# A hybrid decoder layer on one core: the up-projection's products at fixed places in one PSUM pool

## The chip, the core and the metric

The kernel runs on one core of a Trainium2 chip. The metric is the device time of one execution in microseconds (us); lower is better. Five engines work side by side: TensorE (PE, matmuls; PEld is its weight load), VectorE (DVE), ScalarE (ACT), GpSimd (POOL) and SyncE (SP, which issues most DMAs). Each takes its own instructions in order and waits on semaphores that the others raise. Matmuls write to PSUM, which has eight banks of 128 x 512 fp32 values; DVE and ACT read them from there.

## The reference, cut to what matters

A sequence of 1024 tokens of width 1024 goes through one layer: RMSNorm, two attention branches, gates, a residual, and then the part that the change touches, the gated MLP with a causal convolution of width 3 over 2816 hidden channels:

```python
def conv_ffn(xn, w_up, conv_w, conv_b, w_down):
    u = xn @ w_up                                   # (1024, 5632)
    upad = jnp.pad(u, ((0, 0), (CONV_WIDTH - 1, 0), (0, 0)))
    c = conv_b
    for j in range(CONV_WIDTH):
        c = c + upad[:, j:j + S] * conv_w[j]
    gate, val = jnp.split(c, 2, axis=-1)
    return (jax.nn.silu(gate) * val) @ w_down
...
        xn = rmsnorm(x, norm_ffn_w[l])
        x = x + conv_ffn(xn, w_up[l], conv_w[l], conv_b[l], w_down[l])
```

## The kernel before, in words

Everything is held transposed: channels on the 128 partitions, the 1024 tokens along the free axis. An fp32 product is made of three fp32r matmuls: both operands are split into a high part (`...h`, a cast on ACT) and a low part (`...l`, a subtraction on DVE, L145 and L877), and high x high, high x low and low x high are added in PSUM.

The up-projection works on pairs of 128-channel blocks: pair j is gate block j and value block j + 22, for j = 0 to 21. Each pair's 2 x 2 block product is done by a Strassen-like scheme with seven products, P1 to P7, of 12 matmuls of 128x512 each (`product`, L957). The sums of weight blocks that this takes are `sa` and `sb` (made on POOL, L123 to L127), their high and low parts `sh` and `sl`; those of the plain blocks are `wh` and `wl`. The factor of the norm, `rstd`, is applied after the product. It comes from sums of squares (`ssq`, L223), a mean on DVE (`ms`, L230), a power on POOL (`rs`, L232), and eight transposes on PE (`spread`, L238) that bring it to all partitions in PSUM, from where ACT copies it in two halves into `rstd` (L1036).

Three stretches of `hidden` differ in how they hold the products.

- Pair 0 takes eight tiles `t` of one bank each from a pool `psF`: seven products and the sums of squares. `recombine` reads them (L515 to L523): L515 reads P1, L516 P2, L517 P6, L518 P7, L519 and L520 P5, L522 P3, L523 P4.
- Pairs 1 to 19 run in `steady`. `psF` is closed, and two pools take its banks: `psB` (four banks, tile `b`) and `psC` (two tiles `c` of two banks). A pair has three accumulators: b1 takes P1, then S2, S3 and A22 products on top of it; b2 takes P2; b3 takes S1 and S4. ACT copies what is in them between two products (L1108 s1, L1122 u2, L1124 s5 with tile name u, L1136 u3, L1094 or L1082 the last one), so that each product needs the copy before it. The tile of the transposes, `sp`, comes from `psC`. In the built program it lies in the two banks that P3 and P7 of pair 0 had.
- Pairs 20 and 21 take seven banks `t` each from a third pool, `psG2`. In the built program P1 of pair 20 lies in the bank of pair 19's b1.

While PE multiplies pair j, the other engines finish pair j - 1: the scale by `rstd` (L1213), the convolution's first tap on ACT (`taps` with n = 0, L1148, from `us` into a PSUM tile `c`), two taps on DVE (L1150), Silu (L1126), the product of the halves (L1128), and a store to `hd`. They also prepare the weights of pair j + 1. In `steady` the order on DVE, ACT and POOL is the order of the code (`in_order`); on PE and elsewhere a scheduler keeps the code's order as far as the inputs' estimated readiness lets it. With `reuse_waits="tile"` a tile in a reused place waits for the readers of the tiles that lay there.

Of the kernel before, what the change touches and what calls it, by code (L numbers as in the profile page):

```python
# [17 lines left out]
P = 128  # L18
# [26 lines left out]
class Trunk:  # L45
# [914 lines left out]
    def hidden(self, pair):  # L960
        nc, tc = self.nc, self.tc
        with ExitStack() as ctx:
            e = ctx.enter_context
            pctx = ExitStack()
            psF = self.psT = pctx.enter_context(tc.tile_pool(name="psF", bufs=8, space=PSUM, reuse_waits="tile"))
# [8 lines left out]
            for j in (0, NF - 2, NF - 1):  # L974
                w, ps = (ready.pop(j), {}) if j else (w0, {})
                if j == 0:

                    ps = {n: self.tl(psF, [P, H2], "t") for n in ("P1", "P2", "P5", "P7", "", "P6", "P3", "P4")}
                    ssq = ps.pop("")
# [22 lines left out]
                if j:  # L1002
                    ps = {n: self.tl(psF, [P, H2], "t") for n in (("P5", "P1", "P2", "P6", "P7", "P3", "P4") if j < NF - 1 else ("P1", "P2", "P5", "P6", "P7", "P4", "P3"))}
# [15 lines left out]
                if j == 0:  # L1019
# [7 lines left out]
                    pctx.close()  # L1027
                    with tc.tile_pool(name="psB", bufs=4, space=PSUM, reuse_waits="tile") as psB, \
                            tc.tile_pool(name="psC", bufs=2, space=PSUM, reuse_waits="tile") as self.psC:
                        b1, b2 = (self.tl(psB, [P, H2], "b") for _ in range(2))  # L1030
                        self.product(b1, st[1]["w"]["A11"], "B11", skip=True)
                        self.product(b2, st[1]["w"]["A12"], "B21", skip=True)
                        sp = self.tl(self.psC, [P, T], "c")
                        self.spread(sp, rs, 0, NB)
                        for hf in range(2):
                            self.mark_a = nc.scalar.copy(self.rstd[:, hf * H2:(hf + 1) * H2], sp[:, hf * H2:(hf + 1) * H2]).ins  # L1036
                        self.mark_v, self.mark_p = self.lo.ins, self.pow.ins
                        self.front, self.us = None, us
                        st[0] = {"us": us}
                        self.steady(st, (b1, b2), psB, tp, sums)  # L1040
                    psF = self.psT = e(tc.tile_pool(name="psG2", bufs=8, space=PSUM, reuse_waits="tile"))
# [27 lines left out]
    def steady(self, st, banks, psB, tp, sums):  # L1069
# [5 lines left out]
        with self.in_order(last):  # L1075
            c21 = None
            for j in range(1, NF - 1):
# [25 lines left out]
                if j > 1:  # L1103
                    b2 = self.tl(psB, [P, H2], "b")
                    self.product(b2, W["A12"], "B21", skip=True)
# [364 lines left out]
```

## Time and profile before

| | |
|---|---|
| median of 3 runs | 1329.02 us (1328.35 to 1329.96) |
| the profiled execution | 1328.19 us, of it span 1326.4 us |
| mean granted TensorE clock | 0.997 |
| PE busy | 1309.9 us, 99% of the span |
| DVE, ACT, POOL busy | 77%, 50%, 36% |
| PE's share of the chain that ended last | 94% |

The span is the time from the first to the last instruction; times in the order of time count from its start. A row of that order reads: start, duration, engine, line, operation, tile written <- tiles read, shape, and in brackets how long the engine had idled before it and what released it. Matmuls overlap: one of 128x512 is shown with 0.39 us, but the next starts 0.23 us after it. Buffer numbers are left out of names, so `b` is any of b1 to b3.

### The profile page before, as it was taken

The page shows a single profiled execution, that of the slowest core. Times are in us where ns is not written, and L with a number is a line of the kernel's source. Part 1 is how long each engine was busy: PE and PEld are TensorE (multiplying, and loading weights), DVE is VectorE, ACT ScalarE, POOL GpSimd, SP SyncE. Part 2 cuts the span into 40 slices and gives each one's busy share as a digit, 9 for nine tenths or more (in the row PEclk, how much of TensorE's full clock was granted, in tenths as well). Part 3 has the DMA queues.
Part 4 walks back from the last instruction along what each step waited for, and adds up shares of the span by engine and source line. Part 5 has one row for each costly group of instructions (what it writes and reads, how often), then busy time and mean ns, then how long its engine had stood idle before and what let it go on. Part 6 is the DMA issues. An engine that isn't in the chain of part 4 may idle for free.

```text
span 1326.4 us, 16954 instructions
## 1 busy us (share of the span) xinstructions
PE 1309.9 (99%) x6210; PEld 1091.4 (82%) x6210; DVE 1017.6 (77%) x1380; ACT 658.3 (50%) x1043; POOL 473.3 (36%) x364
## 2 busy tenths in 40 slices
PE   9999999999999999999998999999999999999997
PEld 7888888888888878888887888888888888888886
DVE  8846775289888976445668889888988897896865
ACT  9432232276667764333445454545454544554543
POOL 0446652000111015651436568656766632000002
PEclk9999999999999999999999999999999999999999
DMA  7334433976554236334433546745654127954534
GB/s 261 121 144 158 147 146 127 264 185 180 154 128 137 86 128 219 130 111 159 131 108 124 181 135 157 199 148 133 201 134 129 61 87 247 333 190 117 166 98 147
DMA packets 71586, 205.95 MB, mean 155 GB/s; under 512 B 8016, under 2 KB 15824, under 8 KB 71376
## 3 DMA queue, kind: packets, MB, share of 16 engines
q1 hardware_dynamic: 57472, 176.03, 40.8%
q0 software_dynamic: 2304, 11.54, 4.9%
q10 hardware_dynamic: 11728, 17.31, 3.6%
q8 instruction: 49, 0.80, 0.3%
q14 instruction: 33, 0.27, 0.1%
HBM read 156.08 MB, written 71.83 MB: 172 GB/s over the span
## 4 chain that ended last, share of the span: by engine, by line
PE 94%; DVE 2%; ACT 1%; issue 1%; DMA 0%; POOL 0%; SPq 0%; POOLq 0%; ACTq 0%; DVEq 0%
PE b L957 27%; PE t L957 16%; PE y L1283 9%; PE d L1283 7%; PE g L215 4%; PE g L216 4%; PE g L217 4%; PE sc L216 3%; PE sc L215 3%; PE sc L217 3%; PE sc L689 3%; PE t L705 1%; PE t L808 1%; PE sc L777 1%; PE t L717 1%; PE t L798 1%
## 5 line engine op out<-in xcount | busy, mean ns | idle before, releaser
L1213 POOL TENSOR_TENSOR us<-us,rstd 128x1024 f32<-128x1024 f32 x42 | 105.0, 2500 | 148.7 <-DVE us L1138 111.7
L196 DVE TENSOR_TENSOR wl<-raw,wh 128x1024 fp32r<-128x1024 f32 (+2 forms) x85 | 97.4, 1146 | 58.7 <-ACT wh L194 48.9
L194 ACT CAST wh<-raw 128x1024 fp32r<-128x1024 f32 (+2 forms) x85 | 74.2, 874 | 119.9 <-PE y L1283 50.7
L145 DVE TENSOR_TENSOR sl<-sf,sh 128x1024 fp32r<-128x1024 f32 x42 | 106.0, 2525 | 4.6 <-ACT sh L138 4.6
L232 POOL TENSOR_TENSOR rs<-ms,mhalf 128x8 f32<-128x8 f32 (+2 forms) x9 | 13.3, 1474 | 234.4 <-DVE ms L230 228.3
L1150 DVE SCALAR_TENSOR_TENSOR c<-us,vecs,c 128x1024 f32<-128x1024 f32 x76 | 95.6, 1279 | 0.7
L1283 PE MATMUL y<-h,wh 128*128 128x512 f32 (+1 forms) x324 | 95.2, 377 | 0.0
L1283 PE MATMUL d<-h,wh 128*128 128x512 f32 x264 | 81.3, 389 | 0.0
L215 PE MATMUL g<-xh,wh 128*128 128x512 f32 x176 | 71.0, 403 | 1.5 <-ACT g L618 1.5
L216 PE MATMUL g<-xl,wh 128*128 128x512 f32 x176 | 70.3, 400 | 0.0
L217 PE MATMUL g<-xh,wl 128*128 128x512 f32 x176 | 70.3, 399 | 0.0
L1283 PEld LDWEIGHTS y<-h,wh 128*128 128x128 f32 x324 | 59.4, 188 | 11.1
L1283 PE MATMUL y<-h,wl 128*128 128x512 f32 (+1 forms) x162 | 60.9, 376 | 0.0
L693 DVE CUSTOM_DVE_ANT_0 L<-sc,bias 128x128 f32<-128x128 f32 (+7 forms) x64 | 47.7, 752 | 17.0 <-PE sc L689 13.9
L672 POOL MEMSET aT<- 128x128 f32 x32 | 6.2, 206 | 151.7 <-PE t L718 98.0
L694 ACT ACTIVATE L<-L,sm 128x128 f32<-128x128 f32 (+7 forms) x64 | 49.6, 778 | 20.0 <-DVE sm L693 13.5
L1283 PEld LDWEIGHTS d<-h,wh 128*128 128x128 f32 x264 | 49.6, 188 | 10.4
L846 POOL TENSOR_TENSOR gr<-gr,rstd 128x1024 f32<-128x1024 f32 x16 | 40.3, 2520 | 46.7 <-DMA gr<-gd 39.0
L1283 PE MATMUL d<-h,wl 128*128 128x512 f32 x132 | 51.5, 390 | 0.0
L138 ACT CAST sh<-sf 128x1024 fp32r<-128x1024 f32 x42 | 44.3, 1054 | 13.3 <-POOL sf L124 12.0
L216 PE MATMUL sc<-ml,wh 128*128 128x512 f32 x128 | 49.9, 390 | 0.0
L215 PE MATMUL sc<-mh,wh 128*128 128x512 f32 x128 | 49.8, 389 | 0.0
(515 smaller groups left out, 4181.1 us busy)
## 6 DMA issues: line engine op xcount, KB each, us to landing
u<-qd SPq DMA_DIRECT2D x72, 256.0 KB, 6.6
raw<-in_w_up SPq DMA_DIRECT2D x23, 512.0 KB, 3.9
raw<-in_w_in SPq DMA_DIRECT2D x22, 512.0 KB, 3.8
hd<-c SPq DMA_DIRECT2D x22, 512.0 KB, 4.0
sdP<-in_w_down POOLq DMA_DIRECT2D x16, 704.0 KB, 8.6
rv<-in_w_up SPq DMA_DIRECT2D x21, 512.0 KB, 3.6
hc<-hd SPq DMA_DIRECT2D x33, 256.0 KB, 5.1
gr<-gd SPq DMA_DIRECT2D x16, 512.0 KB, 3.7
```

The costliest lines, as they stand in the source:

```text
L145: self.nc.vector.tensor_tensor(lo, src, hi.bitcast(F32), ALU.subtract)
L194: self.hi = nc.scalar.copy(wh, raw)
L196: self.lo = (eng or nc.vector).tensor_tensor(wl, raw, wh.bitcast(F32), ALU.subtract)
L215: nc.tensor.matmul(ps, wh[:, kc + o, :], ah, start=first and n == 0, stop=False)
L216: nc.tensor.matmul(ps, wh[:, kc + o, :], al, start=False, stop=False)
L217: nc.tensor.matmul(ps, wl[:, kc + o, :], ah, start=False, stop=last and n == len(kcs) - 1)
L693: nc.vector.tensor_tensor_reduce(L[:, :w], sc[:, lo:lo + w], self.bias[:, o:o + w], slope, 3e38, ALU.add, ALU.min, s[:, 0:1])
L694: nc.scalar.activation(L[:, :w], L[:, :w], AF.Exp, bias=s[:, 0:1], scale=-1.0, accum_out=s[:, 1:2] if c else self.s0[:, i:i + 1])
L957: nc.tensor.matmul(ps, (ah, ah, al)[p][:, k, :], (bh, bl, bh)[p], start=first and n == p == 0, stop=last and p == 2 and n == len(ks) - 1, ...
L1150: nc.vector.scalar_tensor_tensor(c, us[:, 2 - n:T + 2 - n], cw[2 - n], c, ALU.mult, ALU.add)
L1213: i = (nc.vector if m % NF == 0 else nc.gpsimd).tensor_tensor(us[:, 2:], us[:, 2:], self.rstd, ALU.mult)
L1283: nc.tensor.matmul(ps, v[:, k - k0, :], x, start=start and k == i == 0, stop=k == HK - 1 and i == 2, skip_group_check=True)
```

## The change

One pool, `psF`, with one buffer for each name, serves all 22 pairs. `bank(n)` gives the one-bank tile n0 to n3, and `banks(n)` gives the two halves of the two-bank tile c0 or c1: four banks and two times two. A tile is tracked as a whole, so whoever writes a half of c0 waits for what has read the other half.

- Pair 0: P1 in n0, P2 in n2, P7 in n1, P5 in n3, sums of squares and P6 in c0, P3 and P4 in c1.
- Pairs 1 to 19: b1 alternates between n0 and n1, b2 is n2, b3 is n3; the convolution's tiles are c0 for the gate half and c1 for the value half. The transposes write the two halves of c0, four for each, and ACT copies each half (now L1034).
- Pairs 20 and 21 use the same names. P1 of pair 20 is n1, P4 of it n0, which is pair 19's b1.
- In pair 1 (the second) the taps of pair 0 stand behind copies: the gate half's first tap behind u2 (L1128 in the changed kernel), the value half's behind s5 (L1132).

No instruction's work changes. The number of matmuls, copies, subtractions and DMAs stays.

On PE, pair 0's last two products: `t_6328` holds the sums of squares, `t_6329` is P6; in the changed kernel c_1085 is c0 (sums and P6), c_1086 is c1 (P4 here). Before:

```order
L223 MATMUL t_6328<-ones,rstd 128x1 x3
L957 MATMUL t_6329<-T_0h,sh_6312 128x512 [waits Activation_49]
L957 MATMUL t_6329<-T_0l,sh_6312 128x512 [waits DVE_49]
L957 MATMUL t_6329<-T_0h,sl_6314 128x512
L957 MATMUL t_6329<-T_1h,sh_6312 128x512 [waits Activation_49]
```

After:

```order
L223 MATMUL c_1085_6328<-ones,rstd 128x1 x3
L957 MATMUL c_1086_6329<-T_0h,wh_6320 128x512 [waits Activation_49]
L957 MATMUL c_1086_6329<-T_0l,wh_6320 128x512 [waits DVE_49]
L957 MATMUL c_1086_6329<-T_0h,wl_6322 128x512
L957 MATMUL c_1086_6329<-T_1h,wh_6320 128x512 [waits Activation_49]
L957 MATMUL c_1085_6328<-T_0h,sh_6312 128x512 [waits DVE_49]
L957 MATMUL c_1085_6328<-T_0l,sh_6312 128x512
```

Four matmuls of P4 moved ahead of P6, and P6's first matmul waits for a DVE instruction, which is the mean L230.

On PE, the transposes in pair 1 (`b_6502` is b1, now n_1110; `b_6503` is b2, now n_1111). Before:

```order
L957 MATMUL b_6503<-B_3h,wl_6473 128x512
L238 MATMUL c_6528<-ident,rs_6422 128x128 [waits DVE_49,Pool_49]
L238 MATMUL c_6528<-ident,rs_6422 128x128 x7
L957 MATMUL b_6502<-T_0h,sh_6476 128x512 [waits Activation_49]
L957 MATMUL b_6502<-T_0l,sh_6476 128x512
```

After:

```order
L957 MATMUL n_1111_6494<-B_3h,wl_6471 128x512
L238 MATMUL c_1112_6519<-ident,rs_6420 128x128 [waits DVE_49,Pool_49]
L238 MATMUL c_1112_6519<-ident,rs_6420 128x128 x3
L957 MATMUL n_1110_6493<-T_0h,sh_6474 128x512 [waits Activation_49]
L957 MATMUL n_1110_6493<-T_0l,sh_6474 128x512
L957 MATMUL n_1110_6493<-T_0h,sl_6475 128x512
L957 MATMUL n_1110_6493<-T_1h,sh_6474 128x512
L238 MATMUL c_1112_6519<-ident,rs_6420 128x128 [waits Activation_49]
L238 MATMUL c_1112_6519<-ident,rs_6420 128x128 x3
L957 MATMUL n_1110_6493<-T_1l,sh_6474 128x512
```

The DVE instruction waited for is L522 before and L517 after; four of the transposes moved behind four matmuls and wait for an ACT instruction, the copy of the first half.

On ACT in pair 1, from the cast of the third pair's `sa` on (`c_6558` and `c_6575` are pair 0's convolution tiles, `u_1118` is u2, `u_1119` is s5). Before:

```order
L138 CAST sh_6554<-sf_6492 128x1024 [waits Pool_49]
L1036 COPY rstd<-c_6528 128x512 [waits PE_49]
L1036 COPY rstd<-c_6528 128x512
L1148 ACTIVATE c_6558<-us_6448,vecs 128x1024 [waits DVE_49]
L1148 ACTIVATE c_6575<-us_6449,vecs 128x1024 [waits DVE_49,Activation_49]
L1122 COPY u_1118_6548<-b_6502 128x512 [waits PE_49]
L1124 COPY u_1119_6549<-b_6582 128x512 [waits PE_49]
L1126 ACT_TABLE_LOAD
```

After:

```order
L138 CAST sh_6545<-sf_6490 128x1024 [waits Pool_49]
L1034 COPY rstd<-c_1112_6519 128x512 [waits PE_49] x2
L1128 COPY u_1116_6539<-n_1110_6493 128x512 [waits DVE_49,PE_49]
L1162 ACTIVATE c_1125_6579<-us_6446,vecs 128x1024 [waits DVE_49]
L1132 COPY u_1117_6540<-n_1124_6565 128x512 [waits PE_49]
L1162 ACTIVATE c_1126_6594<-us_6447,vecs 128x1024 [waits DVE_49]
L1140 ACT_TABLE_LOAD
```

Each of the two first taps moved behind one copy. The diff:

```diff
@@ -961,8 +961,7 @@
         nc, tc = self.nc, self.tc
         with ExitStack() as ctx:
             e = ctx.enter_context
-            pctx = ExitStack()
-            psF = self.psT = pctx.enter_context(tc.tile_pool(name="psF", bufs=8, space=PSUM, reuse_waits="tile"))
+            self.psF = e(tc.tile_pool(name="psF", bufs=1, space=PSUM, reuse_waits="tile"))
             xc2 = e(tc.tile_pool(name="xc2", bufs=1, side="right", reuse_waits="tile"))
             self.uw = e(tc.tile_pool(name="uw", bufs=3, side="right", reuse_waits="tile"))
             prods = (("P1", "A11", "B11"), ("P2", "A12", "B21"), ("P5", "S1", "T1"), ("P7", "S3", "T3"),
@@ -975,8 +974,8 @@
                 w, ps = (ready.pop(j), {}) if j else (w0, {})
                 if j == 0:
 
-                    ps = {n: self.tl(psF, [P, H2], "t") for n in ("P1", "P2", "P5", "P7", "", "P6", "P3", "P4")}
-                    ssq = ps.pop("")
+                    ps = {n: self.bank(b) for n, b in (("P1", 0), ("P2", 2), ("P7", 1), ("P5", 3))}
+                    (ssq, ps["P6"]), (ps["P3"], ps["P4"]) = self.banks(0), self.banks(1)
                     for name, a, b in prods[:5]:
                         self.product(ps[name], w[a], b, range(3), last=False)
                     for k in range(4):
@@ -1000,7 +999,10 @@
                             self.hs[k] = self.split(h[:, 0], h[:, 1], raw[k // 2][:, k % 2 * H2:(k % 2 + 1) * H2])
                         lo = self.lo
                 if j:
-                    ps = {n: self.tl(psF, [P, H2], "t") for n in (("P5", "P1", "P2", "P6", "P7", "P3", "P4") if j < NF - 1 else ("P1", "P2", "P5", "P6", "P7", "P4", "P3"))}
+                    o = NF - 1 - j
+                    ps = {n: self.bank(b) for n, b in (("P1", (3, 1)[o]), ("P2", (1, 2)[o]), (("P5", 2), ("P4", 0))[o])}
+                    for i, names in enumerate((("P6", "P7"), ("P4", "P3")) if j == NF - 1 else (("P5", "P6"), ("P7", "P3"))):
+                        ps.update(zip(names, self.banks(i)))
                 for name, a, b in (prods[i] for i in ((0, 1, 2, 5, 3, 6, 4) if j == NF - 1 else (0, 1, 2, 5, 3, 4, 6) if j else (5, 6))):
                     self.product(ps[name], w[a], b, low=name == "P1")
                 us = [self.tl(tp, [P, T + 2], "us", bufs=3) for _ in range(2)]
@@ -1024,21 +1026,16 @@
                         self.whole(st[1], "g", "sa", "sb", "v")
                         st[2] = self.raw_pair(self.wsrc.pop(0)[0])
                         self.sums(st[2], "sa")
-                    pctx.close()
-                    with tc.tile_pool(name="psB", bufs=4, space=PSUM, reuse_waits="tile") as psB, \
-                            tc.tile_pool(name="psC", bufs=2, space=PSUM, reuse_waits="tile") as self.psC:
-                        b1, b2 = (self.tl(psB, [P, H2], "b") for _ in range(2))
-                        self.product(b1, st[1]["w"]["A11"], "B11", skip=True)
-                        self.product(b2, st[1]["w"]["A12"], "B21", skip=True)
-                        sp = self.tl(self.psC, [P, T], "c")
-                        self.spread(sp, rs, 0, NB)
-                        for hf in range(2):
-                            self.mark_a = nc.scalar.copy(self.rstd[:, hf * H2:(hf + 1) * H2], sp[:, hf * H2:(hf + 1) * H2]).ins
-                        self.mark_v, self.mark_p = self.lo.ins, self.pow.ins
-                        self.front, self.us = None, us
-                        st[0] = {"us": us}
-                        self.steady(st, (b1, b2), psB, tp, sums)
-                    psF = self.psT = e(tc.tile_pool(name="psG2", bufs=8, space=PSUM, reuse_waits="tile"))
+                    b1, b2 = self.bank(0), self.bank(2)
+                    self.product(b1, st[1]["w"]["A11"], "B11", skip=True)
+                    self.product(b2, st[1]["w"]["A12"], "B21", skip=True)
+                    for hf, sp in enumerate(self.banks(0)):
+                        self.spread(sp, rs, hf * 4)
+                        self.mark_a = nc.scalar.copy(self.rstd[:, hf * H2:(hf + 1) * H2], sp).ins
+                    self.mark_v, self.mark_p = self.lo.ins, self.pow.ins
+                    self.front, self.us = None, us
+                    st[0] = {"us": us}
+                    self.steady(st, (b1, b2), tp, sums)
                     w21 = st[NF - 1]
                     self.sums(w21, "sb")
                     self.whole(w21, "g", "sa", "sb", "v")
@@ -1066,7 +1063,14 @@
                     else:
                         self.defer.append(f)
 
-    def steady(self, st, banks, psB, tp, sums):
+    def bank(self, n):
+        return self.tl(self.psF, [P, H2], f"n{n}")
+
+    def banks(self, n):
+        t = self.tl(self.psF, [P, 2, H2], f"c{n}")
+        return t[:, 0], t[:, 1]
+
+    def steady(self, st, banks, tp, sums):
 
         nc, tc = self.nc, self.tc
         tt = nc.vector.tensor_tensor
@@ -1089,7 +1093,7 @@
                 if j == 1:
                     b1, b2 = banks
                 else:
-                    b1 = self.tl(psB, [P, H2], "b")
+                    b1 = self.bank((j + 1) % 2)
                     self.product(b1, W["A11"], "B11", skip=True)
                     nc.scalar.copy(half(old[1], 0), c21)
                     self.low(S, "sb")
@@ -1101,27 +1105,37 @@
                 for w in range(2):
                     self.scaled(m + w * NF, old[w])
                 if j > 1:
-                    b2 = self.tl(psB, [P, H2], "b")
+                    b2 = self.bank(2)
                     self.product(b2, W["A12"], "B21", skip=True)
                 s1, u2, s5, u3 = (self.tl(tp, [P, H2], n, bufs=1) for n in ("s1", "u2", "u4", "u3"))
                 us = S["us"] = [self.tl(tp, [P, T + 2], "us", bufs=3) for _ in range(2)]
                 nc.scalar.copy(s1, b1)
                 if j == 1:
                     self.whole(nxt, "sa")
-                c0 = self.taps(m, old[0], 0)
+                c0 = self.taps(m, old[0], 0) if j > 1 else None
                 self.product(b1, W["S2"], "T2", first=False, skip=True)
-                self.taps(m, old[0], 1, c0)
+                if j > 1:
+                    self.taps(m, old[0], 1, c0)
                 tt(half(us[0], 0), b2, s1, ALU.add)
-                self.taps(m, old[0], 2, c0)
-                c1 = self.taps(m + NF, old[1], 0)
-                self.taps(m + NF, old[1], 1, c1)
-                self.taps(m + NF, old[1], 2, c1)
+                if j > 1:
+                    self.taps(m, old[0], 2, c0)
+                    c1 = self.taps(m + NF, old[1], 0)
+                    self.taps(m + NF, old[1], 1, c1)
+                    self.taps(m + NF, old[1], 2, c1)
                 self.sums(nxt, "sb")
-                b3 = self.tl(psB, [P, H2], "b")
+                b3 = self.bank(3)
                 self.product(b3, W["S1"], "T1", skip=True)
                 nc.scalar.copy(u2, b1)
+                if j == 1:
+                    c0 = self.taps(m, old[0], 0)
                 self.product(b1, W["S3"], "T3", first=False, skip=True)
                 nc.scalar.copy(s5, b3)
+                if j == 1:
+                    c1 = self.taps(m + NF, old[1], 0)
+                    for n in (1, 2):
+                        self.taps(m, old[0], n, c0)
+                    for n in (1, 2):
+                        self.taps(m + NF, old[1], n, c1)
                 c = self.tl(self.cpl, [P, T], "c")
                 nc.scalar.activation(c, c0, AF.Silu)
                 self.whole(nxt, "g")
@@ -1144,7 +1158,7 @@
         nc = self.nc
         cw = [self.vecs[:, C_CW + 3 * m + k:C_CW + 3 * m + k + 1] for k in range(3)]
         if n == 0:
-            c = self.tl(self.psC, [P, T], "c")
+            c = self.tl(self.psF, [P, T], f"c{m // NF}")
             nc.scalar.activation(c, us[:, 2:], AF.Identity, bias=self.vecs[:, C_CB + m:C_CB + m + 1], scale=cw[2])
         else:
             nc.vector.scalar_tensor_tensor(c, us[:, 2 - n:T + 2 - n], cw[2 - n], c, ALU.mult, ALU.add)
```

## The prediction

> **What bounds the kernel now.** I read the page's table of engines first, then the list of what TensorE waited for, then the order of time around the two waits that the change touches.
>
> ```profile
> PE 1309.9 (99%) x6210; PEld 1091.4 (82%) x6210; DVE 1017.6 (77%) x1380; ACT 658.3 (50%) x1043; POOL 473.3 (36%) x364
> engine line waited for: us in total, times, longest us
> PE c L238 <- DVE us L522: 3.7, 1, 3.7
> ...
> PE t L957 <- ACT us L1082: 0.7, 1, 0.7
> ```
>
> PE is busy for 99% of the span, so the change can only win what PE idles or runs slowly. That list has ten rows. The first is by far the largest and is in the function that is changed; so is L1082's. No row of it names a product into `b`: the nineteen pairs between run without a wait. So there are two places to win at, and the question is what stands behind each.
>
> The first, in order of time (start, duration, engine, line, tile):
>
> ```profile
> 701.41 0.39 PE L957 MATMUL b<-B_3h,wl 128*128 128x512 f32 x1
> 702.83 0.68 DVE L519 TENSOR_TENSOR us<-t,u 128x512 f32<-128x512 f32 x1
> ...
> 704.63 0.68 DVE L522 TENSOR_TENSOR us<-t,u 128x512 f32<-128x512 f32 x1
> 705.45 1.07 PE L238 MATMUL c<-ident,rs 128*128 128x128 f32 x8 [3.65 <-DVE us L522]
> 706.26 0.69 PE L957 MATMUL b<-T_0h,sh 128*128 128x512 f32 x1
> 706.75 0.63 PE L957 MATMUL b<-T_0l,sh 128*128 128x512 f32 x1
> ...
> 710.46 0.39 PE L957 MATMUL b<-T_3h,sl 128*128 128x512 f32 x1
> 710.69 0.39 PE L957 MATMUL b<-T_0h,sh 128*128 128x512 f32 x1
> ```
>
> A full-speed matmul starts 0.23 us after the one before it (710.46, 710.69; over a row of them 0.2265), so PE could have gone on at 701.63. The eight transposes that spread the norm's factor go into a tile that lies over the banks of P3 and P7 of the first pair, and P3's last reader is L522: PE starts at 705.45. Behind the wait the matmuls start 0.42 to 0.49 us apart. The clock says why (columns: stretch, length, busy time of PE, PEld, DVE, ACT, POOL, granted clock, DMA share, GB/s):
>
> ```profile
> core 0: us, PE busy (x) PEld busy (x) DVE busy (x) ACT busy (x) POOL busy (x), PEclk, DMA share, GB/s
> 699.54:702.95 3.41, 2.26 (x10) 1.53 (x9) 3.41 (x4) 1.88 (x3) 2.33 (x2) 1.00 0.44 154
> 702.95:706.36 3.41, 0.91 (x9) 0.94 (x10) 2.95 (x5) 1.04 (x1) 3.41 (x3) 1.00 0.00 0
> 706.36:709.78 3.41, 3.41 (x11) 2.67 (x10) 2.11 (x2) 1.92 (x3) 0.67 (x1) 0.50 0.64 183
> ```
>
> After a stretch of 3.41 us with PE busy for 0.91 us (27%) the clock is halved for exactly one such stretch; after one with 2.26 us (66%) it was not. The S2 product's twelve matmuls take 710.69 - 706.26 = 4.43 us where 12 x 0.2265 = 2.72 would do: the half clock costs 1.71 us. The place thus costs 3.82 + 1.71 = 5.5 us.
>
> The second place, at the last but one pair:
>
> ```profile
> 1064.08 0.39 PE L957 MATMUL b<-T_3h,wl 128*128 128x512 f32 x1
> 1064.56 0.59 ACT L1082 COPY us<-b 128x512 f32<-128x512 f32 x1 [1.89 <-PE b L957]
> 1065.20 0.50 PE L957 MATMUL t<-B_0h,wh 128*128 128x512 f32 x1 [0.73 <-ACT us L1082]
> 1065.54 0.39 PE L957 MATMUL t<-B_0l,wh 128*128 128x512 f32 x1
> ```
>
> P1 of that pair takes the bank of the accumulator that the copy L1082 has yet to read. PE could have gone on at 1064.31, goes on at 1065.20, and the first matmul after a stop takes 0.34 instead of 0.23 us: 1.0 us.
>
> **The change part by part.** *Place 1, a new wait ahead of it.* The sums of squares and P6 now share one tile, so P6 may only start when the mean (DVE L230) has read the sums. PE puts four matmuls of P4 in front.
>
> ```profile
> 690.66 0.48 PE L957 MATMUL t<-T_0h,sh 128*128 128x512 f32 x1
> 690.98 0.40 PE L957 MATMUL t<-T_0l,sh 128*128 128x512 f32 x1
> 692.31 0.16 DVE L230 TENSOR_SCALAR ms<-t 128x8 f32<-128x8 f32 x1
> ```
>
> The four start at 690.66, 690.98, 691.21 and 691.44; the fifth could start at 691.66. L230 ends at 692.47, and PE follows a DVE result after 0.14 us (705.31 to 705.45 above): 692.61. That is 0.95 us of waiting and 0.1 for the restart, +1.05. DVE's queue ahead of L230 is the same, so the bounds are narrow, 0.9 to 1.15.
>
> *Place 1, the wait removed.* The next products are as many as before, so PE stands before the transposes at 701.63 + 1.05 = 702.68. Their tile now lies over the sums and P6; P6's reader L517 needs P6 (complete near 695.5) and moves behind the first `sl` subtraction, so it ends near 701.0: no wait. The wait for L522 goes.
>
> *Place 1, what is late next.* The transposes are now two groups of four into halves of one tile, and the second group waits until ACT has copied the first half. That copy stands on ACT behind a cast that waits for POOL:
>
> ```profile
> 700.54 1.29 POOL L123 TENSOR_TENSOR sf<-rv 128x512 f32<-128x512 f32 x1 [1.21 <-issue]
> 701.90 2.13 POOL L124 TENSOR_TENSOR sf<-sf,raw 128x512 f32<-128x512 f32 x1
> 704.07 1.04 ACT L138 CAST sh<-sf 128x1024 fp32r<-128x1024 f32 x1 [2.66 <-POOL sf L124]
> 706.56 1.08 ACT L1036 COPY rstd<-c 128x512 f32<-128x512 f32 x2 [1.44 <-PE c L238]
> ```
>
> POOL and DVE ahead of these have the same work, so the cast still ends at 705.11 and the copy (half of 1.08, begun at the cast's end) at 705.62; PE goes on at 705.75. Before that it does four transposes (half of 706.26 - 705.45: 0.41) and four matmuls (0.91), to 704.00. The new wait is 1.75 us. Then 0.41 for four transposes, 0.33 for the matmul after the stop and 7 x 0.2265: the S1 product starts at 708.1 instead of 710.69. Against 3.82 + 0.81 + 4.43 = 9.06 us before stand 0.41 + 0.91 + 1.75 + 0.41 + 1.92 = 5.40, plus the 1.05: a gain of 2.6 us. Bounds: L124 takes 2.13 us where its neighbour takes 1.29; at 1.29 the wait shrinks by 0.84, and a second such slow instruction ahead of it would add 0.84. I take the row as it stands. The sum holds no half clock; the rival below prices that.
>
> *The second pair's order on ACT.* The copies u2 and u4 (L1122, L1124; u4 is the tile of s5) go ahead of the two convolution starts (L1148). Without it the starts, 2.4 us together, would hold u2 back and the S3 product with it; with it u2 is read near 708.9, before S3's turn at 710.8. But the value half's start now stands between u4 and the chain that leads to the third pair's weights:
>
> ```profile
> 708.93 2.41 ACT L1148 ACTIVATE c<-us,vecs 128x1024 f32<-128x1024 f32 x2 [1.29 <-DVE us L1213]
> 713.21 0.39 PE L957 MATMUL b<-T_3h,sl 128*128 128x512 f32 x1
> 713.63 0.59 ACT L1124 COPY u<-b 128x512 f32<-128x512 f32 x1 [1.78 <-PE b L957]
> 714.24 1.28 ACT L1126 ACT_TABLE_LOAD   x1
> 715.53 1.03 ACT L1126 ACTIVATE c<-c 128x1024 f32<-128x1024 f32 x1
> 716.46 1.04 ACT L138 CAST wh<-raw 128x1024 fp32r<-128x1024 f32 x1
> ```
>
> From the last S1 matmul's end: 0.03 to u4, then from start to start 0.61 for u4, 1.2 for the start of the value half, 1.29 for the table, 0.93 for Silu, and 1.04 for the cast, 5.07 us, and 0.13 to PE: 5.23. PE has the 24 matmuls of S3 and S4 to do, 5.44 us less the 0.16 by which a matmul's end lies behind its successor's start: 5.28. The margin was 1.2 us (cast done at 717.50, its product's turn at 713.21 + 25 x 0.2265 = 718.87) and falls to about nothing. I count 0 here and 0 to 1.0 us for the range.
>
> *Nineteen pairs.* Pool and names give each product the bank it had in effect: alternate banks for the first accumulator, one each for the other two. PE's rows and the places at which it waits are the same. Cost 0.
>
> *Place 2.* P1 takes the other accumulator's bank, free since the pair before: -1.0 us. P4, last in the order, takes the bank that L1082 reads. DVE, ACT and SP get another order in the last two pairs; that is covered as long as they have room there, and DVE has:
>
> ```profile
> 1100.00:1110.00 10.00, 10.00 (x46) 8.26 (x45) 6.40 (x9) 3.86 (x5) 0.00 (x0) 1.00 0.41 139
> ```
>
> POOL's order is unchanged, no DMA is added. **Sum: -2.6 - 1.0 = -3.6 us.** The profiled execution took 1328.19 us, 1326.4 of it span; it lies 0.83 below the median of 1329.02. Taken from the median: 1325.4.
>
> **The rivals.** *The clock falls again* (1327.1). The gap of 1.75 us, less the 0.16 in which the last matmul still runs, leaves a stretch of 3.41 us busy for 53% at worst. That is between the 66% that kept the clock and the 27% that halved it; the end of the kernel brings the lower bound up to 43%:
>
> ```profile
> 1317.35:1320.76 3.41, 1.48 (x10) 1.15 (x10) 2.13 (x6) 1.21 (x3) 2.20 (x2) 1.00 0.51 182
> 1320.77:1324.18 3.41, 0.00 (x0) 0.00 (x0) 1.37 (x2) 0.07 (x1) 1.28 (x1) 0.50 1.01 356
> ```
>
> If it falls, 1.71 us come back and the gain is 1.9. For it: 53% lies in the open part, and some of it is transposes. Against it: the stretches lie on a fixed grid (1320.76 is 180 of them after 706.36), and nearly half of the places that the gap can have on it split it over two. [...]
>
> *The third pair waits for its weights* (1326.4). DVE's two convolution steps or POOL's contention make Silu late, and every 0.1 us passes to PE, since the margin is gone. At 1 us the gain is 2.6.
>
> *One bank is too few* (slower, 1332). The S1 accumulator has one fixed bank; if its reader were late, each of 18 pairs would wait, and 0.35 us in each would undo 3.6 us and add 2.7.
>
> ```profile
> 719.80 0.68 DVE L1138 TENSOR_TENSOR us<-b,u 128x512 f32<-128x512 f32 x1
> 729.75 0.39 PE L957 MATMUL b<-T_0h,sh 128*128 128x512 f32 x1
> ```
>
> The reader ends at 720.48, the next product into it starts at 729.75: DVE would have to be 9 us later. Little speaks for it.
>
> *The wait only moves* (1328.7). The first copy ends near 705.6 whatever PE does; if POOL's sum lands 2.5 us later still, place 1 gains nothing and place 2 is eaten by a late P1.
>
> **How the numbers follow.** Forecast 0.54, clock 0.27, third pair 0.10, moved wait 0.05, slower 0.04. About 0.2%, 2.7 us, is what a measurement here can tell from no change, so faster means below 1326.4. The forecast is 1.0 us beyond that and counts as faster for 0.52 of its 0.54, the third pair for half; the clock and the moved wait are "same". Faster 0.57, same 0.39, slower 0.04. The range goes from 1323.8 (L124 at 1.29 us, and the runs' own 0.7 below the median) to 1328.0 (the clock rival and 0.9 above).
>
> **What would show it.** In the profile after: no wait of L238 for L522 but one of about 1.75 us of the transposes' second group for ACT's copy, near 704 to 706; a wait of about 1 us for L230 near 692; full clock between 706 and 710; no wait where L1082 stood; no wait in the products of the pairs between. The prediction is wrong if the clock is halved again, if the third pair's first product waits for its cast, or if a wait appears in the pairs between.

## The result, and the profile after

The changed kernel takes **1324.88 us** (median of 7 runs, 1324.45 to 1326.47); the kernel before, in 7 runs beside it, 1328.58 us (1328.06 to 1329.96). The ratio is 0.9972, 95% interval 0.9961 to 0.9984: 3.70 us less, where 3.6 was forecast.

The page's row of the engines, after:

```profile
PE 1309.5 (99%) x6210; PEld 1091.5 (82%) x6210; DVE 1015.8 (77%) x1380; ACT 658.5 (50%) x1043; POOL 471.8 (36%) x364
```

From the list of what TensorE waited for (in total, times, longest), after:

```profile
engine line waited for: us in total, times, longest us
PE c L238 <- ACT rstd L1034: 1.5, 1, 1.5
...
PE c L957 <- DVE ms L230: 0.7, 1, 0.7
```

Both rows of before that the prediction built on are gone: no wait of the transposes (L238) for L522, none for the copy in the tail. Two new ones stand for them, and there is still none in the products of pairs 2 to 19. The busy times hardly differ, as no instruction's work changed.

The first place in order of time, TensorE after (start, duration, engine, line, tile, shape, idle time before it and its releaser):

```profile
692.29 0.48 PE L957 MATMUL c<-T_0h,wh 128*128 128x512 f32 x1
...
693.07 0.39 PE L957 MATMUL c<-T_1h,wh 128*128 128x512 f32 x1
694.15 0.50 PE L957 MATMUL c<-T_0h,sh 128*128 128x512 f32 x1 [0.70 <-DVE ms L230]
...
704.03 0.39 PE L957 MATMUL n<-B_3h,wl 128*128 128x512 f32 x1
704.26 0.60 PE L238 MATMUL c<-ident,rs 128*128 128x128 f32 x4
704.61 0.48 PE L957 MATMUL n<-T_0h,sh 128*128 128x512 f32 x1
...
705.39 0.40 PE L957 MATMUL n<-T_1h,sh 128*128 128x512 f32 x1
707.32 0.65 PE L238 MATMUL c<-ident,rs 128*128 128x128 f32 x4 [1.53 <-ACT rstd L1034]
...
709.65 0.39 PE L957 MATMUL n<-T_0h,sh 128*128 128x512 f32 x1
```

The four matmuls of P4, then a stop for the mean; the first four transposes right behind P2's last matmul; then four matmuls of S2, a stop, the other four transposes; S1 starts at 709.65. What the second stop waits for, on GpSimd and ScalarE:

```profile
703.54 2.15 POOL L124 TENSOR_TENSOR sf<-sf,raw 128x512 f32<-128x512 f32 x1
705.73 1.04 ACT L138 CAST sh<-sf 128x1024 fp32r<-128x1024 f32 x1 [2.40 <-POOL sf L124]
706.68 0.58 ACT L1034 COPY rstd<-c 128x512 f32<-128x512 f32 x1
```

GpSimd's sum, the cast that waits for it, and only then the copy that empties the first half of the tile: the copy ends at 707.26, TensorE goes on at 707.32.

In this profiled execution (1326.47 us, the longest of the seven) the first matmul behind the sums of squares starts at 692.29 us of the span, before at 690.66. The change lies wholly behind it, so places are compared by their distance from it. The table gives that distance, for the first matmul of each product, in every kernel that was profiled; "weights" is the first product of the third pair, which needs that pair's weights, and "down" the first matmul of the down-projection. The kernels e1 to e10 are those of the experiments below.

| kernel | transposes | S2 | S1 | S3 | weights | down |
|---|---|---|---|---|---|---|
| before | 14.79 | 15.61 | 20.03 | 22.77 | 28.21 | 412.76 |
| after | 11.98 | 12.33 | 17.37 | 20.09 | 25.53 | 409.07 |
| e1_tail_undone | 12.00 | 12.35 | 17.35 | 20.07 | 25.51 | 410.07 |
| e2_fill_gap | 14.79 | 15.61 | 18.44 | 21.23 | 26.81 | 411.37 |
| e3_swap_c | 16.59 | 17.14 | 21.86 | 24.58 | 30.02 | 413.54 |
| e4_old_order | 12.01 | 12.37 | 17.36 | 20.55 | 26.15 | 409.67 |
| e5_p4_split | 11.76 | 12.36 | 17.79 | 20.51 | 25.95 | 409.47 |
| e5_again | 11.76 | 12.36 | 17.77 | 20.49 | 25.93 | 409.45 |
| e10_p4_split_filled | 12.34 | 12.69 | 17.80 | 20.52 | 25.96 | 409.50 |
| e6_spread_first | 11.97 | 12.76 | 15.59 | 18.31 | 25.03 | 408.71 |
| e7_cast_early | 12.00 | 12.79 | 15.62 | 18.34 | 23.78 | 408.01 |
| e8_silu_later | 11.98 | 12.77 | 15.61 | 18.33 | 26.49 | 407.29 |

In e8 the last product of the second pair (A22, 12 matmuls) stands ahead of the third pair's first one and starts at 23.77, so its "weights" can't be compared with the others.

From before to after, 2.66 us are won up to S1, 2.68 up to the third pair, and 3.69 up to the down-projection.

### The profile page after: what moved, and what is told of

It reads as the page before. It is cut to its first block, busy times and chain, and to the rows that moved or that the text cites. A ratio compares the mean times of both kernels' runs of the same rounds, so it can differ in the third digit from the quotient of the medians.

```text
span 1324.7 us, 16948 instructions
## 1 busy us (share of the span) xinstructions
PE 1309.5 (99%) x6210; PEld 1091.5 (82%) x6210; DVE 1015.8 (77%) x1380; ACT 658.5 (50%) x1043; POOL 471.8 (36%) x364
## 4 chain that ended last, share of the span: by engine, by line
PE 95%; DVE 2%; DMA 1%; ACT 1%; POOL 1%; issue 1%; POOLq 0%; ACTq 0%; SPq 0%; DVEq 0%
PE n L957 28%; PE t L957 13%; PE y L1297 9%; PE d L1297 7%; PE g L215 4%; PE g L216 4%; PE g L217 4%; PE sc L215 3%; PE sc L217 3%; PE sc L216 3%; PE sc L689 3%; PE c L957 2%; PE t L705 1%; PE t L808 1%; PE t L341 1%; PE t L342 1%
## 5 line engine op out<-in xcount | busy, mean ns | idle before, releaser
L689 PE MATMUL sc<-u,u 128*128 128x512 f32 (+2 forms) x192 | 50.0, 359 | 0.1
```

Of the source, the lines that this page charges most:

```text
L689: nc.tensor.matmul(sc[:, lo + n0:lo + n1], qs, k[c][part][:, n0:n1], start=part == 0, stop=part == 1)
```

## Experiments: is the sum made of the two places?

**The tail put back (e1).** The changed kernel, with pair 20's P1 in the bank of pair 19's b1 again; TensorE's order of that pair's products is held by lines that are not shown:

```diff
-(("P1", (3, 1)[o]), ("P2", (1, 2)[o]), (("P5", 2), ("P4", 0))[o])
+(("P1", (3, 0)[o]), ("P2", (0, 2)[o]), (("P5", 2), ("P4", 1))[o])
```

> The changed kernel with P1 of pair 20 put back into the bank of pair 19's last accumulator, and the products of that pair held in the order P1, P2, ... Theory (place 2 is worth 1.0 us by the bank and the order together): PE waits for the last copy of pair 19 again, about 0.7 us of idle time near 1063 and 1.0 us in all, and the time is the changed kernel's plus 1.0, near 1325.9. Rival (place 2 was hidden, and the whole 3.7 us came from place 1): the wait is there, but the end does not move, 1324.9.

Measured: 1325.14 us (1324.90 to 1325.65), ratio to before 0.9975 (0.9966 to 0.9985). Its profile has the wait of before back:

```profile
1060.99 0.39 PE L957 MATMUL n<-T_3h,wl 128*128 128x512 f32 x1
1062.11 0.50 PE L957 MATMUL n<-B_0h,wh 128*128 128x512 f32 x1 [0.73 <-ACT us L1088]
```

1062.11 - 1060.99 = 1.12 us where 0.23 would do, and 0.11 more for the restart: 1.00. The table says the same (410.07 against 409.07). The medians, 3.00 us below the kernel before in this series against 3.70 in the other, lean the same way, but the intervals are wider than what lies between theory and rival, and 1325.14 taken by itself lies nearer the rival's 1324.9, in a series in which the kernel before took 0.44 us less too; the traces decide for the theory.

**The gap filled, nothing removed (e2).** The kernel before, with the second pair's P2 done twice: 2.72 us more work in the place where TensorE idles.

```diff
 self.product(b2, st[1]["w"]["A12"], "B21", skip=True)
+self.product(b2, st[1]["w"]["A12"], "B21", skip=True)
```

> The kernel before with the P2 product of pair 1 done twice in a row ahead of the transposes: twelve matmuls, 2.72 us, that leave the result as it is and fill most of the 3.82 us in which PE waited for L522. Theory (the half clock after the wait comes of PE's idling and costs 1.7 us): the transposes start when they did, the clock stays at 1.00, the S2 product takes 2.7 us instead of 4.43, and since the copy u2 then stands behind the two convolution starts on ACT, the S3 product waits 0.2 to 0.3 us for it: 1.4 to 1.7 us faster than before, near 1327.1. Rival (the matmuls there are slow for another reason, such as their operands): they take 0.43 us each again and the time is that of before, 1328.6.

Measured: 1326.54 us, beside 1328.14 for the kernel before: 1.60 less, ratio 0.9986 (0.9976 to 0.9995). Busy time and clock (as in the prediction: stretch, length, PE, PEld, DVE, ACT, POOL, granted clock) on this run's grid:

```profile
701.38:704.79 3.41, 2.48 (x12) 1.75 (x11) 3.41 (x6) 1.05 (x1) 3.41 (x3) 1.00 0.05 18
704.79:708.21 3.42, 3.42 (x20) 2.96 (x21) 1.67 (x3) 1.07 (x2) 1.56 (x1) 1.00 0.57 156
```

The clock stays at 1.00, and S2 takes 18.44 - 15.61 = 2.83 us instead of 4.42. More work made the kernel faster, so the half clock and not the wait alone was part of the price: 1.59 us at S1 by the table. At the down-projection 1.39 of it are left (411.37 against 412.76): the S3 product then waits for the copy u2, as was expected, and with the restart that costs 0.2. The medians' 1.60 fits both.

**The two double banks exchanged (e3).** The changed kernel, with pair 0's P3 and P4 in c0, where the transposes go:

```diff
-(ssq, ps["P6"]), (ps["P3"], ps["P4"]) = self.banks(0), self.banks(1)
+(ps["P3"], ps["P4"]), (ssq, ps["P6"]) = self.banks(0), self.banks(1)
```

> The changed kernel with one thing undone: in pair 0, P3 and P4 lie in c0 and the sums with P6 in c1, so that the transposes' tile waits for P3's and P4's readers (L522, L523) again. Theory (place 1 is that wait and its half clock): PE idles 4 to 4.7 us ahead of the transposes, the clock is halved for 3.4 us behind it, and the time is 4.0 to 4.7 us above the changed kernel's, near 1329.3, somewhat above before, since the wait for the mean has stayed. Rival (place 1 came from the second pair's order on ACT, or from the products' order): within 1 us of the changed kernel, near 1325.

Measured: 1328.64 us beside 1328.14 for the kernel before, ratio 1.0001 (0.9992 to 1.0011). The third pair starts 4.49 us later than in the changed kernel (30.02 against 25.53). TensorE's longest wait, and the stretches:

```profile
PE c L238 <- DVE us L523: 4.4, 1, 4.4
```

```profile
703.47:706.88 3.41, 0.20 (x2) 0.23 (x3) 3.03 (x5) 1.04 (x1) 2.90 (x2) 1.00 0.53 160
706.88:710.29 3.41, 3.41 (x13) 2.90 (x12) 0.00 (x0) 0.69 (x2) 0.00 (x0) 0.50 0.95 342
```

The transposes wait for L523, the last reader of the products that now lie under them, and the clock falls behind that wait. So what one pool gains at this place hangs on which products the transposes' tile follows; with the names the other way round the whole change is worth nothing.

**The old order in the second pair (e4).** The changed kernel, with pair 0's taps ahead of the copies u2 and s5 again:

```diff
-c0 = self.taps(m, old[0], 0) if j > 1 else None
+c0 = self.taps(m, old[0], 0)
...
-if j == 1:
-    c0 = self.taps(m, old[0], 0)
```

> The changed kernel with the second pair's convolution back in its old order, ahead of the copies u2 and s5. Theory (that order is cover and not the gain): the S3 product waits 0.4 to 0.7 us for u2, the rest stays, 0.3 to 0.7 us above the changed kernel, near 1325.4. Rival (the order carries most of the gain): near before, 1328. Second rival (the order does nothing): no wait of the S3 product and the changed kernel's time, 1324.9.

Measured: 1325.06 us (1324.78 to 1326.00), ratio 0.9977 (0.9967 to 0.9987). TensorE's list has a row for the S3 product:

```profile
PE n L957 <- ACT u L1126: 0.3, 1, 0.3
```

S3 starts 3.19 us behind S1 instead of 2.72, and the third pair 0.62 us later than in the changed kernel. In the profile the new order is worth 0.6 us; the medians (3.08 us below the kernel before in this series, against 3.70) agree with that, but their intervals overlap.

## Experiments: what sets the second stop, and what stands behind it?

**P6 later, so that it need not wait for the mean (e5).** The changed kernel, in pair 0:

```diff
+self.product(ps["P4"], w["A22"], "T4", range(3), last=False)
+self.product(ps["P6"], w["S2"], "T2")
+self.product(ps["P4"], w["A22"], "T4", (3,), first=False)
...
-if j else (5, 6)
+if j else ()
```

> The changed kernel, with one edit in the first pair: P6 comes behind the third step of P4 instead of ahead of P4, so TensorE no longer waits for the mean's copy (L230, 0.70 us in the changed kernel's profile). Theory, that the chain L124 on GpSimd, cast of sh on ScalarE, first copy of rstd sets the moment at which S1 starts: TensorE comes to the transposes 0.7 us earlier, waits there for VectorE's L517 (about 1.4 us where there was no wait), S2 is done as late as before, and the first matmul of the third pair stands where it stood, within 0.1 us: time equal to the changed kernel's, 1324.9 +- 0.4, ratio to the kernel before 0.9972. A longer idle stretch there (1.4 and 1.0 us close together) might also halve the clock again: then +1.0 to +1.7 us, with a half-clock stretch to be seen. Rival, that waits of TensorE simply add up: 0.7 us less, 1324.2.

Measured: 1326.26 us (1324.57 to 1328.24), ratio 0.9983 (0.9974 to 0.9992). The wait for the mean is gone, and nothing was won:

```profile
PE c L238 <- ACT rstd L1038: 1.9, 1, 1.9
...
PE c L238 <- DVE u L517: 0.6, 1, 0.6
```

The stop at the transposes is longer and one for L517 is new; the third pair starts 0.42 us later than in the changed kernel. The rival's -0.7 is out. The theory's "within 0.1" was too narrow, and VectorE and GpSimd show why:

```profile
699.55 2.60 DVE L145 TENSOR_TENSOR sl<-sf,sh 128x1024 fp32r<-128x1024 f32 x2 [6.60 <-ACT sh L138]
702.07 0.68 DVE L517 TENSOR_TENSOR u<-c,s 128x512 f32<-128x512 f32 x1
702.67 1.16 DVE L145 TENSOR_TENSOR wl<-rv,wh 128x512 fp32r<-128x512 f32 x1
...
701.02 2.26 POOL L123 TENSOR_TENSOR sf<-rv 128x512 f32<-128x512 f32 x1 [1.21 <-issue]
703.36 1.62 POOL L124 TENSOR_TENSOR sf<-sf,raw 128x512 f32<-128x512 f32 x1
```

L123 starts at 701.02, while VectorE subtracts until 702.15, and takes 2.26 us instead of the 1.30 it takes in the changed kernel; L124 starts 0.47 us before the end of another subtraction (703.83) and takes 1.62 instead of 2.15. Together they take 3.88 us against 3.45, and those 0.43 us are the 0.42 by which the third pair is late. In each case the time left behind the end of the other engine's instruction is 1.13 and 1.15 us, near the 1.29 that each of GpSimd's three sums from 694.65 to 698.43 takes in the same run, with VectorE idle (6.60 us ahead of 699.55). So the two sums are longer by about the 1.13 and 0.47 us that they lie beside a subtraction, to about 0.15 us; by what the one engine holds the other up no run shows, and none took the neighbour of these two away.

**The same kernel again (e5 again), and the same with the gap filled (e10).** The median of 1326.26 lay above what its own trace explains. One idea was the clock, falling in some of its executions. So the kernel ran again, beside one in which half of the second pair's P2 is done in addition:

```diff
+self.product(b2, st[1]["w"]["A12"], "B21", range(2), last=False, skip=True)
 self.product(b2, st[1]["w"]["A12"], "B21", skip=True)
```

> The kernel with P6 behind three steps of P4, a second time: its ten executions had a median of 1326.26, though the profiled one (1325.33) had the first matmul of the third pair only 0.42 us later than the changed kernel and its end level with it. Theory: its two waits (0.62 and 1.89 us, 1.6 us apart) lie on the clock's grid of 3.41 us so that one stretch is busy for 45% here and less in other executions, and in some of them the clock is halved for 3.41 us (+1.7 us): executions in two heaps, near 1325.2 and 1326.8, median 1325.3 to 1326.5; if the profiled one is of the upper heap, it shows a half-clock stretch. Rival: nothing of the place, the median was high by chance: 1325.0 to 1325.4, one heap.

> The same kernel with the first six matmuls of the second pair's P2 done twice (1.36 us of useless work, started over afterwards), which fills the first of the two waits, so that no stretch is less than about 50% busy. The copy of rstd, which ends last, does not move. Theory (the clock): one heap, 1325.0 to 1325.4, about 1 us below the same kernel without them, though it does more work; no half-clock stretch. Rival (not the clock): the median of the same kernel without them, or above it.

Measured: 1324.95 us again (1324.08 to 1326.09; ratio 0.9976, 0.9966 to 0.9985) and 1324.69 with the gap filled (1324.16 to 1326.03; ratio 0.9975, 0.9964 to 0.9985). There is no second heap: but for one execution of each, all took 1324.08 to 1325.30. Neither trace has the clock at half at this place (1.00 in every stretch from 698.4 to 712.0 us), and the place is worth nothing: in all three traces the third pair starts 0.40 to 0.43 us later than in the changed kernel. That 1.36 us of extra matmuls cost nothing (25.96 against 25.93) says once more that TensorE is not what sets the moment here: L124, the cast and the copy do.

Why the first median was higher (2.29 us below the kernel before in its series, 3.12 in this one) stays open. The three traces are of executions of 1325.33, 1324.51 and 1324.29 us and can't show what a long one had. The mean granted clock of each execution leans towards the idea: in the first series the four at 0.996 took 1326.38 to 1328.24 us and the six others 1324.57 to 1326.33; in the second the only one at 0.996 is the longest. One more stretch at half clock would lower the mean by 0.5 x 3.41 / 1323 = 0.0013. But the mean doesn't say where the clock was low, and in e1 two executions at 0.996 (1325.10 and 1325.51) were no longer than the rest.

**All eight transposes first (e6).** The changed kernel, with both groups ahead of the two copies, so that the second needs no emptied half:

```diff
+sps = self.banks(0)
+for hf, sp in enumerate(sps):
     self.spread(sp, rs, hf * 4)
+for hf, sp in enumerate(sps):
     self.mark_a = nc.scalar.copy(...)
```

> The changed kernel, with the eight transposes of a normalisation issued before either copy of rstd, so that the second four need no bank which the first copy must empty (two banks instead of one; the wait `c L238 <- ACT rstd L1034`, 1.53 us, goes). Theory, that the third pair's weights stand right behind it: S1 starts 1.5 us earlier, but the cast of wh (it ended 0.27 us before the third pair's first matmul) stays where ScalarE's order leaves it, and TensorE waits about 1.5 us for it instead: gain 0.0 to 0.3 us, 1324.6 to 1324.9; the wait `n <- ACT wh L138` of about 1.5 us shows in the list. Rival, that the weights follow because ScalarE is ahead of its work: gain 1.5 to 1.75 us, 1323.2.

Measured: 1325.28 us (1323.57 to 1325.83), ratio 0.9971 (0.9962 to 0.9981). The stop of 1.53 us is gone, S1 starts 1.78 us earlier (15.59 against 17.37), and the third pair waits for its weights:

```profile
716.65 0.50 PE L957 MATMUL n<-B_0h,wh 128*128 128x512 f32 x1 [1.12 <-ACT wh L138]
```

On ScalarE that cast stands behind Silu, and Silu waits for VectorE's taps (L1166):

```profile
714.64 1.03 ACT L1142 ACTIVATE c<-c 128x1024 f32<-128x1024 f32 x1 [1.25 <-DVE c L1166]
715.56 1.03 ACT L138 CAST wh<-raw 128x1024 fp32r<-128x1024 f32 x1
```

Of the 1.78 us only 0.50 are left there, 0.36 at the down-projection, and none in the median (3.27 us below the kernel before in its series). The theory holds, with a wait of 1.12 instead of about 1.5 us.

**The cast ahead of Silu (e7).** In addition, for the second pair:

```diff
+if j == 1:
+    self.cast(nxt, "g")
 nc.scalar.activation(c, c0, AF.Silu)
+if j == 1:
+    self.low(nxt, "g")
+else:
+    self.whole(nxt, "g")
-self.whole(nxt, "g")
```

> As the kernel with all transposes first, and for the second pair the cast of the third pair's wh moved on ScalarE ahead of the Silu (a table load of 1.28 us and 1.03 us of work). Theory: the wait for the cast goes, and the next behind it is the fourth product of the third pair, whose bank u3's copy (now 1 us later, behind Silu) must empty: about 0.9 us of wait there; net gain 0.6 to 1.0 us, 1323.9 to 1324.3. Rival, that S1's gain is kept whole once the cast is early: 1.6, 1323.3.

Measured: 1323.95 us (1323.37 to 1324.74), ratio 0.9966 (0.9952 to 0.9980). The weights are in time (23.78: all of the 1.75 us), and the next thing is late, the copy u3 behind Silu. The product that waits for it is the second pair's own last one, A22, and not one of the third pair as was expected:

```profile
PE n L957 <- ACT u L1157: 0.4, 1, 0.4
```

1.06 us remain at the down-projection, just above the theory's 0.6 to 1.0.

**Silu behind u3 as well (e8).** What follows the cast (Silu, the low part, the product of the halves, the store) is put into `finish`:

```diff
+if j == 1:
+    self.cast(nxt, "g")
+else:
+    finish()
...
 nc.scalar.copy(u3, b1)
+if j == 1:
+    finish()
```

> As the last one, and for the second pair Silu with its table load comes behind the last copy of the pair (u3) on ScalarE, so that neither the cast nor a copy stands behind it. Theory: nothing is left to wait for at the second pair's end, and the gain of the transposes is kept: 1.5 to 1.75 us less than the changed kernel, 1323.0 to 1323.4, ratio to the kernel before about 0.9960. Rival, that the gain meets a later thing (the product c of the pair that comes 2.5 us later, the fourth pair's sums, or a second table load where Silu is split from the copies): 0.5 to 1.0 only.

Measured: **1323.05 us** (1322.54 to 1324.42), ratio to before 0.9960 (0.9947 to 0.9972). ScalarE and TensorE at the place:

```profile
702.15 1.03 PE L238 MATMUL c<-ident,rs 128*128 128x128 f32 x8
702.94 0.47 PE L957 MATMUL n<-T_0h,sh 128*128 128x512 f32 x1
...
710.57 1.04 ACT L138 CAST wh<-raw 128x1024 fp32r<-128x1024 f32 x1
711.51 0.58 ACT L1161 COPY u<-n 128x512 f32<-128x512 f32 x1
712.10 1.28 ACT L1143 ACT_TABLE_LOAD   x1
713.40 1.03 ACT L1143 ACTIVATE c<-c 128x1024 f32<-128x1024 f32 x1
```

Between the sums and the down-projection TensorE waits for nothing but the mean, and the down-projection starts 1.78 us earlier than in the changed kernel: the whole of what e6 won at S1. The forecast of 1.5 to 1.75 stands. TensorE's own order moved along with the edit (A22 ahead of the third pair's first product, as under the table); the cast is done at 711.61 and the copy u3 at 712.09, both ahead of S4's end, but whether the old order would have run without a stop too, no run shows. This version beats both: 5.50 us below the kernel before in the same series, 1.8 below the changed one by the trace.

## Why the prediction was right

- *P6 waits for the mean: +1.05.* The mean ends 1.81 us behind the first matmul after the sums, as in before. TensorE could have gone on at 693.30 and went on at 694.15: 0.85, where the forecast had 0.95. The transposes start at 11.98 instead of 10.97: +1.01.
- *The wait for L522 goes, no wait for L517.* So it is: 704.26 stands 0.23 us behind 704.03. e3 shows the wait come back when the products change places.
- *What is late next: 1.75 us at the second group.* TensorE could have gone on at 705.62 and went on at 707.32: 1.70. The row's 1.53 counts from the end that the profile gives the matmul (705.39 + 0.40). The forecast took it as it stood that L124 needs its long time again, 2.13 us before, and that held: 2.15. e5 shows what it hung on. In before and after, VectorE has one of the readers of pair 0's products (L518, now L517) between its two subtractions; in e5 it has none there, they stand closer, and the chain takes 0.43 us more. (The forecast's 705.62 for the copy's end is 0.03 less than its own terms give, 705.11 + 0.54.)
- *The half clock goes.* It does, and in e1 and e4, which have the same second stop, it stays away too (granted clock 1.00 in every stretch from 697.7 to 714.1 us). Its 1.71 us held a restart of 0.1; e2 measures 1.6.
- *Place 1 in all: 2.6.* S1 starts 2.66 us earlier.
- *The second pair's order: 0, no margin left for the third pair's weights.* TensorE runs on without a stop at 717.82, and the cast ends at 717.55:

```profile
716.51 1.04 ACT L138 CAST wh<-raw 128x1024 fp32r<-128x1024 f32 x1
...
717.82 0.40 PE L957 MATMUL n<-B_0h,wh 128*128 128x512 f32 x1
```

  A margin of 0.27 us; the forecast's numbers leave 0.18 (its 0.05, and the 0.13 that it counts from the cast's end to TensorE). That it is so small is what ate e6's gain. What the prediction said would happen without the new order, u2 held back and S3 with it, is 0.6 us in e4.
- *Place 2: -1.0.* 3.69 - 2.68 = 1.01, and e1 gives 1.00 back. In the changed kernel the product simply follows:

```profile
1063.05 0.39 PE L957 MATMUL n<-T_3h,wl 128*128 128x512 f32 x1
1063.28 0.39 PE L957 MATMUL n<-B_0h,wh 128*128 128x512 f32 x1
```

- *The clock rival* (1327.1) did not come about. The worst stretch at the place, on this run's grid, and the end of the kernel:

```profile
702.38:705.79 3.41, 3.41 (x18) 2.48 (x16) 3.41 (x4) 0.82 (x3) 3.33 (x3) 1.00 0.37 137
705.79:709.20 3.41, 1.89 (x11) 1.62 (x12) 3.38 (x6) 2.06 (x3) 2.84 (x2) 1.00 0.52 156
1313.36:1316.77 3.41, 2.38 (x21) 2.21 (x19) 1.59 (x5) 1.93 (x5) 1.81 (x1) 1.00 0.00 0
1316.77:1320.18 3.41, 1.12 (x4) 0.72 (x4) 2.65 (x5) 0.37 (x1) 1.59 (x2) 0.50 0.98 346
```

  55% busy, close to the forecast's worst of 53%, and the clock stayed. That it would, the forecast's argument by the busy share could not secure: it gave the rival 0.27, and a busier stretch lost the clock at the end of this same run. See the last section.
- *Third pair waits, one bank too few, the wait only moves:* none was seen in the changed kernel; the first of them was one step away (e6).
- *The level.* 3.6 us were taken from 1329.02, the median of three runs; beside the changed kernel the kernel before took 1328.58. So the forecast of 1325.4 came out 0.5 too high, while the difference fits to 0.1.

## What to carry to other kernels

Price a removed wait by the next thing that is late there, in every engine's order, and go on one step further: here L522's wait left a copy behind GpSimd's sum, behind that stood the next weights, behind those a copy behind Silu, and only with the last of them moved did TensorE keep what the transposes' order won. When banks are named by hand, lay a tile over those whose last reader is earliest; the same pool with two names exchanged was worth nothing. And look behind a long wait of the matmul engine for a lowered clock (here 1.59 us behind a wait of 3.65 us, in before): useless matmuls in the gap, as in e2, are a cheap test for it.

## What the runs showed of the hardware that was not expected

- *The busy share does not decide alone when the clock falls.* At the first place it fell behind stretches that were 6% (e3) and 27% (before) busy and stayed behind 45% (e5, the first row below), 53% (e5 again and e10), 55% (after), 60% (e1, the second row) and more. But at the end of the changed kernel, in the rows above, it fell behind a stretch that was 70% busy, of narrower matmuls (128x256, 128x128 and 128x1), and at the end of e4 behind one of 61% (the last two rows). The prediction's lower bound of 43% came from that end too, and so was no bound for the first place. What the chip counts, no run here settles. The stretches of 3.41 us lie on a grid that starts elsewhere in each execution, so the same idle time is split differently from run to run. In before, the first matmuls of 128x512 start 0.42 to 0.60 us apart and from 6.61 us of the span on 0.23 to 0.25; in after, the closer starts come from 9.73 on (the trace's record of the clock has the rise at 6.63 and at 9.47). The later changes of the clock (706.36, 709.78 and 1320.76 in before, 1316.77 in after) each come a whole number of stretches of 3.413 us behind the one ahead: 205, 1 and 179, and 383.
```profile
704.70:708.12 3.42, 1.53 (x9) 1.36 (x10) 2.56 (x5) 2.12 (x3) 2.74 (x3) 1.00 0.86 321
```

```profile
703.95:707.36 3.41, 2.06 (x11) 1.81 (x12) 3.38 (x6) 1.88 (x3) 2.66 (x2) 1.00 0.59 185
```

```profile
1312.11:1315.52 3.41, 2.08 (x18) 1.92 (x17) 1.75 (x5) 1.67 (x4) 1.94 (x2) 1.00 0.07 27
1315.52:1318.93 3.41, 1.11 (x4) 0.71 (x4) 2.46 (x4) 0.37 (x1) 1.76 (x2) 0.50 0.93 329
```

- *VectorE's subtractions and GpSimd's sums stretch each other* where they overlap at the first place: GpSimd's sum from 1.29 us (after, at 695.79, VectorE idle) to as much as 2.28 (e10, at 699.95), VectorE's subtraction of 128x1024 from 1.22 (after, at 717.71, GpSimd idle) to 1.99 (after, at 702.56). The one that starts second is the longer: in after the sums that start while a subtraction runs (703.54, 705.66) take 2.15 and 1.72 us, the subtractions of 128x1024 that start while a sum runs (700.70, 702.56) 1.34 and 1.99, and the sums that ran already (699.66, 702.17) keep their 1.30. Moving a matmul product by one place thereby changed a chain on other engines by 0.4 us.
